# Plain weight rows only in the middle FFN stages, five of them and sooner; the next stage's first weights loaded at fixed places

## The chip, the cores and the metric

The kernel runs on one core of one Trainium2 chip. The metric is device time in microseconds of one execution; lower is better. TensorE (PE) multiplies, VectorE (DVE) and ScalarE (ACT) work on tiles in on-chip memory, GpSimd (POOL) and SyncE (SP) mostly issue transfers here. Each of these engines works through its own instructions in order, so an instruction that waits holds up all behind it on the same engine.

## The reference

A trunk of two layers over 512 tokens of width 1024, in float32. Each layer is an FFN, a mixing stage, and a second FFN, every one with its own RMS norm and its own shift, scale and gate computed from a vector c:

```python
for l in range(DEPTH):
    mod = (c_act @ w_ada[l] + b_ada[l]).reshape(B, N_MOD, D_MODEL)
    sh1, sc1, gt1, sh2, sc2, gt2, sh3, sc3, gt3 = [mod[:, i, None, :] for i in range(N_MOD)]
    hn = rms_norm(h, g_ffn1[l]) * (1.0 + sc1) + sh1
    h = h + 0.5 * (1.0 + gt1) * swiglu(hn, w_ffn1_in[l], w_ffn1_out[l])
    hn = rms_norm(h, g_mix[l]) * (1.0 + sc2) + sh2
    proj = hn @ w_mix_in[l]
    ...
    h = h + (1.0 + gt2) * mixed
    hn = rms_norm(h, g_ffn2[l]) * (1.0 + sc3) + sh3
    h = h + 0.5 * (1.0 + gt3) * swiglu(hn, w_ffn2_in[l], w_ffn2_out[l])
```

The FFN's hidden width is 2816: `swiglu(x) = (silu(gate) * up) @ w_out`. The mixing stage (attention in windows, a recurrent part, a short convolution) is not touched by the change, only the moments at which its first weights arrive.

## The kernel before

Activations lie transposed, features on the 128 partitions and the 512 tokens along the row. The six stages run one behind the other: FFN 1, mixing and FFN 2 of layer 0, then of layer 1. Every matmul is made three times in a reduced format: `split` (line 107 on ScalarE, line 108 on VectorE) turns a float32 tile into a high part `wH` and a low part `wL`, and TensorE adds up high by high, high by low and low by high. So each weight tile costs a load, a ScalarE copy and a VectorE subtraction before TensorE can use its last third.

The first FFN goes another way. The other three (second FFN of layer 0, first and second of layer 1) are made by `ffn_whole`, which cuts the weight matrix and the activations in two by two blocks and computes seven block products in place of eight. The first part of the stage takes eleven pairs of hidden blocks one by one (`pair_in`). The second part, `out_product`, multiplies the 22 hidden blocks by `w_out`; its seven products are, in order, A0, S, A1, S0, S1, S3 and A3, and each takes eleven rows of weights, in six units of two, two, two, two, two and one row. A row is 128 partitions by 512 numbers, 256 KB; a unit of two rows is 24 matmuls of 128 x 256 (four output blocks, two rows, three parts), so a row is 12 and a product 132. In the text "product five" is S1, "product six" is S3.

Four of the seven need sums of blocks. S is the sum of two blocks: SyncE loads the first (`sum`), GpSimd adds the second to it with an accumulating transfer. S0 adds A0's rows on VectorE. S1 adds a third block to S's buffers by another accumulating transfer, once S0's splits have read them. S3 adds a block to A0's kept rows (`rowk`), again by accumulating transfers of 256 KB each, with one exception: for the last three rows (8, 9, 10) the block is loaded plainly by SyncE (`Y`, line 836; its place in the table of due times is unit 20 of 42, line 912), and VectorE adds it at line 878, just ahead of that row's split. These are the "plain rows". Where the additions come in VectorE's own order is decided by the program's scheduler, and it may be well ahead of the split.

Loads are issued from a table: `dues` names the unit at which a load is issued, `prepare(t)` issues what is due and makes the splits of the unit two further on, `queued` holds the loads of one engine in that order. `wraw` is a pair of buffers through which loads pass to be split; `com`, `raw`, `sum` and others are buffers of the first part that come free.

Two of these three stages are followed by another one, whose first four weight tiles (W0 to W3 here) are loaded while `out_product` ends: two into `wraw`, one into a part of `spare`, the fourth into a buffer with the tag `raw` (named `wraws`, line 1044). The norm's statistics (`stats`, `spread`: a sum over partitions by TensorE, `ps_ss`, a root, and a broadcast) are woven into the last units of products six and seven; in this place the order of VectorE and ScalarE is written out by hand. The mixing stage then loads weights through `wraw` and, on GpSimd's queue, blocks of `w_ada` (`wada`) and a copy of silu(c) (`crow`), from which VectorE computes dot products (line 171) for later shifts and scales. ScalarE there makes `qr` and `qsq` from finished products, and TensorE's `ps_q` waits for the last of them.

Of the kernel before, what the change touches and what calls it, by code (L numbers as in the profile page):

```python
# [8 lines left out]
F32 = mybir.dt.float32  # L9
# [7 lines left out]
P = 128  # L17
# [46 lines left out]
def trunk_kernel(ctx, tc, ins, out, layers=L, phases=("ffn1", "mix", "ffn2")):  # L64
# [592 lines left out]
    def ffn_whole(l, w_in, w_pair, w_s, hn, im, ss, need, then, ready):  # L657
# [4 lines left out]
        with tc.tile_pool(name="act", bufs=1) as ap_:  # L662
# [65 lines left out]

            crow = []
# [5 lines left out]
            def pair_in(p):  # L735
# [19 lines left out]
                nc.gpsimd.dma_start(a00, A(1, 0), accum_op=ALU.add)  # L755
                if alone:
# [47 lines left out]

            def out_product(rest):
# [5 lines left out]
                tall = [slice(2 * u, min(2 * u + 2, NP)) for u in range(NU)]  # L811
                size = [s.stop - s.start for s in tall]
                S_, kept, late_rows, ready_, chain = {}, {}, {}, {}, {}

                def queued(eng, *args, **kw):
                    with queue_behind(chain.get(eng)):
                        chain[eng] = eng.dma_start(*args, **kw)
# [7 lines left out]
                def load(name, u):  # L825
# [6 lines left out]
                    elif name == "S3":  # L832
                        for k in ks:
                            if k not in late_rows:
                                queued(nc.gpsimd, kept[k], block(one(k), 1, 0), accum_op=ALU.add)
                    elif name == "Y":
                        for k in range(NP - 3, NP):
                            late_rows[k] = row_tile(k)
                            queued(nc.sync, late_rows[k], block(one(k), 1, 0))
                        return  # L840
# [3 lines left out]
                    if name == "A1":  # L844
                        w = wp.tile([P, KD, P], F32, name="wraw", tag="wraw", bufs=2)
                        queued(nc.sync, w[:, :n], block(tall[u], 0, 1))
                    elif name in ("S", "A3"):
                        if u < 5:
                            w = ap_.tile([P, KD, P], F32, name="sum", tag=("sum1", "crep", "first", "sum0", "third")[u], bufs=1)
                        else:  # L850
                            w = hnp.tile([P, 4, P], F32, name="rowk", tag="hn")
                        queued(nc.sync, w[:, :n], block(tall[u], 1, name == "A3"))
                        if name == "S":
                            S_[u] = w
                            queued(nc.gpsimd, w[:, :n], block(tall[u], 1, 1), accum_op=ALU.add)
# [1087 lines left out]
```

## Time and profile before

| | us |
|---|---|
| three runs | 1884.57, 1883.04, 1878.89 |
| median | 1883.04 |
| profiled execution | 1887.26 |
| its span, first to last instruction | 1885.5 |
| mean granted TensorE clock | 0.990 of full |
| out_product of the second FFN of layer 0 | about 835 to 955 |
| out_product of the first FFN of layer 1 | about 1170 to 1290 |
| out_product of the second FFN of layer 1 (last) | about 1755 to 1886 |

All places in the trace are microseconds from the span's start. A row of a list of waits reads: engine, tile and line that waited, what it waited for, the sum, how often, the longest. A row of a timeline: start, length, engine, line, operation, output and inputs, shape, and in square brackets the idle time ahead of it with what ended it. A row of a table by stretches: the stretch, its length, busy time of PE, PE's weight loads, DVE, ACT and POOL with instructions in brackets, then the granted clock, the mean share of the 16 DMA engines, and GB/s. DMA rows in a chain of waits run from issue to arrival. A row of one engine's name with q behind it is the time to issue.

### The profile page before, as it was taken

What the parts mean: (1) busy time and instruction counts of PE and PEld (TensorE: products, weight loads), DVE (VectorE), ACT (ScalarE), POOL (GpSimd) and SP (SyncE); (2) the same over time, 40 slices, a digit from 0 to 9 for tenths busy, and PEclk for the clock granted to TensorE, in tenths of its full rate; (3) what the DMA queues carried; (4) which work ended last, traced back from release to release, by engine and by line L of the source; (5) the groups of instructions that cost most, each with busy time, mean ns of one, the idle gap of its engine ahead of it and who ended that gap; (6) DMA issues with size and microseconds to landing.
All of it is one profiled execution on the core that took longest, in us unless ns stands there. A gap on an engine that the chain in (4) does not pass through costs nothing.

```text
span 1885.5 us, 39610 instructions
## 1 busy us (share of the span) xinstructions
PE 1836.2 (97%) x16468; PEld 1747.0 (93%) x16468; DVE 1538.5 (82%) x2443; ACT 919.7 (49%) x1413; POOL 185.8 (10%) x274
## 2 busy tenths in 40 slices
PE   9999999999999999999999999999999999999979
PEld 8998899888889999999999999999777999999979
DVE  6897687868886889999888998887597778877875
ACT  4453255346342545555654555564553335555544
POOL 0101110100000011110211111021000001110120
PEclk8999999999999999999999999999999999999989
DMA  8666876541212488876738987572211317765772
GB/s 315 215 201 227 273 198 220 187 149 46 75 44 87 132 266 262 256 211 179 177 111 271 267 252 214 172 185 106 88 54 49 103 51 221 199 168 132 199 177 92
DMA packets 112212, 322.01 MB, mean 171 GB/s; under 512 B 24096, under 2 KB 29216, under 8 KB 111008
## 3 DMA queue, kind: packets, MB, share of 16 engines
q1 hardware_dynamic: 74880, 192.06, 29.1%
q0 software_dynamic: 37152, 127.42, 27.6%
q8 instruction: 129, 2.11, 0.4%
q14 instruction: 51, 0.42, 0.1%
HBM read 315.50 MB, written 3.93 MB: 169 GB/s over the span
## 4 chain that ended last, share of the span: by engine, by line
PE 72%; DVE 16%; DMA 7%; issue 2%; ACT 2%; SPq 0%; DVEq 0%; ACTq 0%; POOL 0%; POOLq 0%
PE ps_mm L104 14%; PE ps_d L724 5%; PE ps_d L726 5%; PE ps_d L725 5%; PE ps_d L931 5%; PE ps_mm L97 4%; PE ps_mm L96 4%; PE ps_mm L98 4%; DVE wL L108 3%; DMA rowk<-in_w2s 3%; PE ps_f L724 2%; PE ps_f L725 2%; PE ps_f L726 2%; PE ps_g L931 2%; PE ps_f L931 2%
## 5 line engine op out<-in xcount | busy, mean ns | idle before, releaser
L107 ACT CAST wH<-wraw 128x1024 fp32r<-128x1024 f32 (+2 forms) x210 | 207.1, 988 | 318.6 <-PE ps_f L725 58.3
L108 DVE TENSOR_TENSOR wL<-wraw,wH 128x1024 fp32r<-128x1024 f32 (+2 forms) x210 | 238.7, 1140 | 54.1 <-ACT wH L107 53.7
L107 ACT CAST wH<-sum 128x1024 fp32r<-128x1024 f32 x153 | 161.0, 1052 | 141.0 <-PE ps_d L725 62.6
L108 DVE TENSOR_TENSOR wL<-sum,wH 128x1024 fp32r<-128x1024 f32 x153 | 186.7, 1220 | 36.4 <-ACT wH L107 35.5
L104 PE MATMUL ps_mm<-hnH,wL 128*128 128x256 f32 x976 | 199.1, 282 | 1.3 <-DVE wL L108 1.3
L104 PE MATMUL ps_mm<-hnH,wH 128*128 128x256 f32 x976 | 198.2, 283 | 0.5 <-ACT wH L107 0.3
L104 PE MATMUL ps_mm<-hnL,wH 128*128 128x256 f32 x976 | 196.7, 281 | 0.0
L726 PE MATMUL ps_d<-comH,wL 128*128 128x256 f32 x648 | 179.0, 276 | 0.6 <-DVE wL L108 0.6
L724 PE MATMUL ps_d<-comH,wH 128*128 128x256 f32 x648 | 179.2, 277 | 0.0
L725 PE MATMUL ps_d<-comL,wH 128*128 128x256 f32 x648 | 178.9, 276 | 0.0
L104 PEld LDWEIGHTS ps_mm<-hnH,wH 128*128 128x128 f32 x976 | 149.0, 188 | 9.8 <-issue 6.8
L104 PEld LDWEIGHTS ps_mm<-hnH,wL 128*128 128x128 f32 x976 | 149.7, 189 | 6.7 <-issue 4.6
L104 PEld LDWEIGHTS ps_mm<-hnL,wH 128*128 128x128 f32 x976 | 149.4, 189 | 5.9 <-issue 5.8
L931 PE MATMUL ps_d<-xs,wH 128*128 128x256 f32 x792 | 135.5, 276 | 0.0
L726 PEld LDWEIGHTS ps_d<-comH,wL 128*128 128x128 f32 x648 | 121.6, 188 | 0.8 <-DVE wL L108 0.8
L724 PEld LDWEIGHTS ps_d<-comH,wH 128*128 128x128 f32 x648 | 121.6, 188 | 0.2
L725 PEld LDWEIGHTS ps_d<-comL,wH 128*128 128x128 f32 x648 | 121.7, 188 | 0.0
L931 PEld LDWEIGHTS ps_d<-xs,wH 128*128 128x128 f32 x792 | 119.3, 188 | 0.0
L931 PE MATMUL ps_d<-xs,wL 128*128 128x256 f32 x396 | 109.7, 277 | 4.0 <-DVE wL L108 4.0
L931 PE MATMUL ps_f<-xs,wH 128*128 128x256 f32 x528 | 93.2, 281 | 0.0
L171 DVE SCALAR_TENSOR_TENSOR raw<-raw,crow 128x1024 f32<-128x1024 f32 x68 | 82.7, 1216 | 6.0 <-DMA raw<-in_wadaT 4.9
L171 DVE SCALAR_TENSOR_TENSOR wada<-wada,crep 128x1024 f32<-128x1024 f32 x60 | 71.8, 1220 | 17.2 <-DMA wada<-in_wadaT 17.2
(550 smaller groups left out, 5590.7 us busy)
## 6 DMA issues: line engine op xcount, KB each, us to landing
raw<-in_wadaT POOLq DMA_DIRECT2D x68, 512.0 KB, 6.4
wada<-in_wadaT POOLq DMA_DIRECT2D x60, 512.0 KB, 4.9
wraw<-in_wmi SPq DMA_DIRECT2D x38, 512.0 KB
wraw<-in_w2p SPq DMA_DIRECT2D x36, 512.0 KB
wraw<-in_w1p SPq DMA_DIRECT2D x32, 512.0 KB
sum<-in_w2s SPq DMA_DIRECT2D x20, 512.0 KB
sum<-in_w2s POOLq DMA_DIRECT2D x20, 512.0 KB, 9.1
wraw<-in_w1i SPq DMA_DIRECT2D x18, 512.0 KB
```

Of the source, the lines that this page charges most:

```text
L96: mm(acc, wH, xH, start=start, stop=False)
L97: mm(acc, wH, xL, start=False, stop=False)
L98: mm(acc, wL, xH, start=False, stop=stop)
L104: mm(acc[:, sl], w[a][:, k], x[b][:, sl], start=start and n == 0 and sl is HALVES[0], stop=stop and n == 2, skip_group_check=True)
L107: nc.scalar.copy(hi, src)
L108: return nc.vector.tensor_sub(lo, src, hi.bitcast(F32))
L171: stt(w, w, 1.0, crep, ALU.mult, ALU.mult, accum_out=out_)
L724: mm(pt[:, i], wH, x[k][0], start=start and i + k == 0, stop=False, skip_group_check=True)
L725: mm(pt[:, i], wH, x[k][1], start=False, stop=False, skip_group_check=True)
L726: last = mm(pt[:, i], wL, x[k][0], start=False, stop=k == 3, skip_group_check=True)
L931: mm(pt[m // 2][:, m % 2], w[:, 4 * k + m], x[:, y, k], start=start and u + k + n + m % 2 == 0, stop=u == NU - 1 and n == 2, skip_group_ch ...
```

## The change

1. Plain rows. The last stage has none now: all eleven rows of S3 come by accumulating transfers. The two stages in the middle have five (rows 6 to 10): rows 8, 9 and 10 are due at unit 8, rows 6 and 7 together in one `wraw` buffer at unit 16. Before, all three stages had three, at unit 20.
2. The sums for the first two units of S are issued in the last input pair (`sum_of`) instead of after it; the buffers of the five sums change places.
3. A1's units 2 and 3 get two buffers of `com` instead of waiting for `wraw`; all of A1's due times are new.
4. The next stage's first weights have fixed places in the order: W2 at unit 10, W0 at unit 17, W1 two units before the end of product six, W3 two units after it. W3 goes through `wraw`, no longer through `raw`.
5. `stats` and `spread` of the first half come one unit later.

VectorE's order in the last stage, from the end of S0's splits to S1's second, first before:

```order
L108 TENSOR_TENSOR xs<-raw,xs 128x512
L108 TENSOR_TENSOR wL<-sum,wH 128x1024
L108 TENSOR_TENSOR xs<-raw,xs 128x512 x2
L108 TENSOR_TENSOR wL<-rowk,wH 128x512
L108 TENSOR_TENSOR xs<-raw,xs 128x512
L878 TENSOR_TENSOR rowk<-rowk 128x512 x3
L108 TENSOR_TENSOR wL<-sum,wH 128x1024
L108 TENSOR_TENSOR xs<-raw,xs 128x512
L108 TENSOR_TENSOR wL<-sum,wH 128x1024
```

and now:

```order
L108 TENSOR_TENSOR xs<-raw,xs 128x512
L108 TENSOR_TENSOR wL<-sum,wH 128x1024
L108 TENSOR_TENSOR xs<-raw,xs 128x512 x2
L108 TENSOR_TENSOR wL<-rowk,wH 128x512
L108 TENSOR_TENSOR xs<-raw,xs 128x512
L108 TENSOR_TENSOR wL<-sum,wH 128x1024
L108 TENSOR_TENSOR xs<-raw,xs 128x512
L108 TENSOR_TENSOR wL<-sum,wH 128x1024
```

The three additions of plain rows are gone from between S0's last split (`wL<-rowk`) and S1's first.

SyncE's order in the second FFN of layer 0, from A1's loads to the next stage's weights (`in_w1i`), first before:

```order
L817 DMA wraw<-in_w2s 128x1024 x2
L308 DMA raw<-in_w1i 128x1024
L817 DMA wraw<-in_w2s 128x1024 x3
L817 DMA wraw<-in_w2s 128x512
L817 DMA rowk<-in_w2s 128x512 x3
L308 DMA wraw<-in_w1i 128x1024 x2
L817 DMA sum<-in_w2s 128x1024 x5
L817 DMA rowk<-in_w2s 128x512
L308 DMA wraw<-in_w1i 128x1024 x2
L308 DMA wraws<-in_w1i 128x1024
```

and now:

```order
L815 DMA wraw<-in_w2s 128x1024 x4
L815 DMA rowk<-in_w2s 128x512 x3
L815 DMA raw<-in_w1i 128x1024
L815 DMA wraw<-in_w2s 128x1024
L815 DMA wraw<-in_w2s 128x512
L815 DMA wraw<-in_w2s 128x1024
L815 DMA wraw<-in_w1i 128x1024
L815 DMA sum<-in_w2s 128x1024 x5
L815 DMA rowk<-in_w2s 128x512
L815 DMA wraw<-in_w1i 128x1024 x2
```

The three plain rows (`rowk` x3) moved ahead of A1's last two units, a transfer for rows 6 and 7 (the third `wraw<-in_w2s`) came in behind those, and only one of the next stage's `wraw` loads is now ahead of A3's sums instead of two.

VectorE at the start of layer 1's mixing stage, from W3's split (`wraws` before), first before:

```order
L108 TENSOR_TENSOR wL<-wraws,wH 128x1024
L295 SCALAR_TENSOR_TENSOR hnL<-hn_t,mod_3_9410,hnH 128x256
L1158 TENSOR_SCALAR om<-par 128x8
L1159 TENSOR_SCALAR w0h<-par 128x2
L1160 TENSOR_SCALAR a0h<-par 128x2
L1161 TENSOR_TENSOR gqk<-par 128x1
L108 TENSOR_TENSOR wL<-wraw,wH 128x1024
L1184 RECIPROCAL rk<-rk 128x512
L171 SCALAR_TENSOR_TENSOR wada_15646,mod_7_13740<-wada_15646,crow_15645 128x1024
```

and now:

```order
L108 TENSOR_TENSOR wL<-wraw,wH 128x1024
L295 SCALAR_TENSOR_TENSOR hnL<-hn_t,mod_3_9410,hnH 128x256
L171 SCALAR_TENSOR_TENSOR wada_15650,mod_7_13742<-wada_15650,crow_15649 128x1024
L108 TENSOR_TENSOR wL<-wraw,wH 128x1024
L171 SCALAR_TENSOR_TENSOR wada_15651,mod_7_13742<-wada_15651,crow_15649 128x1024
L1213 RECIPROCAL rk<-rk 128x512
```

The first dot product over `wada`, which needs `crow`, now stands ahead of the second weight split instead of behind it.

The diff, cut to its core:

```diff
-    def load_w(src, n=KD, raw=None, pair=None):
+    def load_w(src, n=KD, raw=None, pair=None, here=False):
...
-        loads.append(nc.sync.dma_start(w[:, :n], src))
+        if not here:
+            loads.append(nc.sync.dma_start(w[:, :n], src))
...
-    def ffn_whole(l, w_in, w_pair, w_s, hn, im, ss, need, then, ready):
+    def ffn_whole(l, w_in, w_pair, w_s, hn, im, ss, upcoming, then, ready):
...
                 nc.gpsimd.dma_start(a00, A(1, 0), accum_op=ALU.add)
+                if p == NP - 1:
+                    for u in range(2):
+                        sum_of(u)
...
+            def sum_of(u):
+
+                n, src = 4 * size[u], [w_s[l, 1, kh, :, tall[u]].rearrange("p k m c -> p (k m) c") for kh in range(2)]
+                if u < 5:
+                    S_[u] = ap_.tile([P, KD, P], F32, name="sum", tag=("sum1", "third", "crep", "first", "sum0")[u], bufs=1)
+                else:
+                    S_[u] = hnp.tile([P, 4, P], F32, name="rowk", tag="hn")
+                queued(nc.sync, S_[u][:, :n], src[0])
+                queued(nc.gpsimd, S_[u][:, :n], src[1], accum_op=ALU.add)
+                ready_["S", u] = [S_[u][:, :n]]
...
+                    elif name == "Y" and u < 4:
+                        w = wp.tile([P, KD, P], F32, name="wraw", tag="wraw", bufs=2)
+                        queued(nc.sync, w[:, :n], block(tall[u], 1, 0))
+                        late_rows.update((k, w[:, 4 * m : 4 * m + 4]) for m, k in enumerate(ks))
+                        return
                     elif name == "Y":
-                        for k in range(NP - 3, NP):
+                        for k in ks:
                             late_rows[k] = row_tile(k)
                             queued(nc.sync, late_rows[k], block(one(k), 1, 0))
+                        return
+                    elif name == "W":
+                        early[u] = wp.tile([P, KD, P], F32, name="wraw", tag="wraw", bufs=2) if u != 2 else flat(spare[3]).rearrange("p (k c) -> p k c", c=P)
+                        queued(nc.sync, early[u], upcoming[u])
...
                     if name == "A1":
-                        w = wp.tile([P, KD, P], F32, name="wraw", tag="wraw", bufs=2)
+                        pool, tag, bufs = (ap_, "com", 8) if u in (2, 3) else (wp, "wraw", 2)
+                        w = pool.tile([P, KD, P], F32, name="wraw", tag=tag, bufs=bufs)
...
-                dues = {-6: [("A0", u) for u in range(3)] + [("S", u) for u in range(3)] + [("A0", 3), ("S", 3)] + [("A0", 4), ("A0", 5), ("S", 4), ("S", 5)]}
+                early = {}
+                dues = {-6: [("A0", u) for u in range(3)] + [("S", 2)] + [("A0", 3), ("S", 3)] + [("A0", 4), ("A0", 5), ("S", 4), ("S", 5)]}
...
-                    due = 0 if name == "A1" and u < 2 else min(t - ahead_of[name], 6 * NU - 3)
+                    due = {0: 0, 1: 0, 2: 6, 3: 6}.get(u, t - 4) if name == "A1" else min(t - ahead_of[name], 6 * NU - 3)
...
-                dues.setdefault(20, []).insert(0, ("Y", 0))
+                if upcoming:
+                    for t, *what_ in ((8, ("Y", 4), ("Y", 5)), (10, ("W", 2)), (16, ("Y", 3)), (17, ("W", 0))):
+                        dues.setdefault(t, []).extend(what_)
...
                 with tc.manual_schedule(engines=HAND):
+                    load("W", 1)
                     prepare(end - 2)
-                    ahead(0, raws[0])
+                    ahead(0, early[0], True)
...
-                    ahead(2, raws[2])
-                    stats(hi_)
+                    ahead(2, early[2], True)
                     prepare(end + 1)
                     nothing(end + 1)
-                    spread(hi_)
+                    stats(hi_)
+                    load("W", 3)
                     prepare(end + 2)
                     nothing(end + 2)
+                    spread(hi_)
...
-                    raws.append(ap_.tile([P, 2, KD, P], F32, name="wraws", tag="raw", bufs=NU)[:, 0])
...
-                    ahead(3, raws[3])
+                    ahead(3, early[3], True)
...
-                marks = ffn_whole(l, ins[w + "i"], ins[w + "p"], ins[w + "s"], hn, im, nss, need, then, ready)
+                marks = ffn_whole(l, ins[w + "i"], ins[w + "p"], ins[w + "s"], hn, im, nss, first_weights(n + 1) if nss else (), then, ready)
```

`upcoming` is the list of the next stage's first four weight tiles; it is empty in the last stage, so the plain rows and the W loads are left out there.

More of the change, by code (lines that the diff above doesn't have):

```diff
@@ L727, in prod @@
                 return last
+            tall = [slice(2 * u, min(2 * u + 2, NP)) for u in range(NU)]
+            size = [s.stop - s.start for s in tall]
             crow = []
@@ L803, in pair_in, with queued @@
                 waiting.append(rest)
+            S_, chain, ready_ = {}, {}, {}
+            def queued(eng, *args, **kw):
+                with queue_behind(chain.get(eng)):
+                    chain[eng] = eng.dma_start(*args, **kw)
+            def sum_of(u):
[7 more added lines that the diff above has]
+                ready_["S", u] = [S_[u][:, :n]]
             def out_product(rest):
@@ L810, in out_product @@
                 pD, pF, pG = ([psum([P, 2, H2], n, t) for _ in range(2)] for n, t in (("ps_d", "x"), ("ps_f", "mm"), ("ps_g", "r0")))
[L811 to L817, printed above, removed]
+                kept, late_rows = {}, {}
                 def block(ks, mh, kh):
@@ L844, in load @@
                     if name == "A1":
-                        w = wp.tile([P, KD, P], F32, name="wraw", tag="wraw", bufs=2)
+                        pool, tag, bufs = (ap_, "com", 8) if u in (2, 3) else (wp, "wraw", 2)
+                        w = pool.tile([P, KD, P], F32, name="wraw", tag=tag, bufs=bufs)
                         queued(nc.sync, w[:, :n], block(tall[u], 0, 1))
-                    elif name in ("S", "A3"):
+                    elif name == "A3":
                         if u < 5:
-                            w = ap_.tile([P, KD, P], F32, name="sum", tag=("sum1", "crep", "first", "sum0", "third")[u], bufs=1)
+                            w = ap_.tile([P, KD, P], F32, name="sum", tag=("sum1", "third", "crep", "first", "sum0")[u], bufs=1)
                         else:
                             w = hnp.tile([P, 4, P], F32, name="rowk", tag="hn")
[L852 to L855, printed above, removed]
+                        queued(nc.sync, w[:, :n], block(tall[u], 1, 1))
                     else:
@@ L1000, in out_product @@
                 silu = im == 6
-                raws = [wp.tile([P, KD, P], F32, name="wraw", tag="wraw", bufs=2) for _ in range(2)]
-                raws.append(flat(spare[3]).rearrange("p (k c) -> p k c", c=P))
                 def update(q, ms):
@@ L1022, in out_product @@
                 with tc.manual_schedule(engines=HAND):
+                    load("W", 1)
                     prepare(end - 2)
-                    ahead(0, raws[0])
+                    ahead(0, early[0], True)
                     prepare(end - 1)
-                    ahead(1, raws[1])
+                    ahead(1, early[1], True)
                     nothing(end - 2)
@@ L1665, in normed, with first_weights @@
         return norm(l, g, im, im + 1, ss, n > 1 and seq[n - 1][1] != "mix")
+    def first_weights(n):
+        l, p = seq[n]
+        if p == "mix":
+            return [ins["wmi"][l, k] for k in range(4)]
+        return [ins["w1i" if p == "ffn1" else "w2i"][l, *divmod(k, 2)] for k in range(4)]
     def begin(pool):
@@ L1836, in then @@
             scale()
-            l2, p2 = seq[n + 1]
-            if p2 == "mix":
-                srcs = [ins["wmi"][l2, k] for k in range(4)]
-            else:
-                srcs = [ins["w1i" if p2 == "ffn1" else "w2i"][l2, *divmod(k, 2)] for k in range(4)]
-            return steps + [lambda k, raw: ws.append(load_w(srcs[k], KD, raw))]
+            srcs = first_weights(n + 1)
+            return steps + [lambda k, raw, here=False: ws.append(load_w(srcs[k], KD, raw, None, here))]
         if p == "mix":
```

3 lines of the change are left out of this document (added).

## The prediction

> **What bounds the kernel now.** I read the page first. TensorE is busy nearly everywhere, so only its gaps, and stretches at a lower clock, can give time back.
>
> ```profile
> PE 1836.2 (97%) x16468; PEld 1747.0 (93%) x16468; DVE 1538.5 (82%) x2443; ACT 919.7 (49%) x1413; POOL 185.8 (10%) x274
> ```
>
> Then I asked for TensorE's waits in the three stages that the diff touches and at the start of the mixing stage behind one of them. First the last stage (1750 to 1886 us):
>
> ```profile
> PE ps_f L931 <- DVE wL L108: 9.8, 2, 9.5
> PE ps_d L931 <- DVE wL L108: 0.8, 1, 0.8
> PE ps_g L931 <- DVE wL L108: 0.7, 2, 0.4
> ```
>
> One wait of 9.5 us stands out; the rest of the three rows is 0.3 + 0.8 + 0.7 = 1.8 us. It stands at the start of product five (S1, into `ps_f`). VectorE's timeline shows why `wL` was late, SyncE's and the chain of waits what it waited for:
>
> ```profile
> 1826.95 0.69 DVE L878 TENSOR_TENSOR rowk<-rowk 128x512 f32<-128x512 f32 x1 [8.87 <-DMA rowk<-in_w2s]
> 1831.55 1.22 DVE L108 TENSOR_TENSOR wL<-sum,wH 128x1024 fp32r<-128x1024 f32 x1
> 1814.79 3.70 SPq L817 DMA_DIRECT2D rowk<-in_w2s  x3
> 1816.82 14.10 DMA rowk<-in_w2s
> 1832.82 17.93 PE ps_f L931 x130
> 1850.75 9.29 PE ps_d L931 x82
> ```
>
> VectorE works in order. The three additions of plain rows (one row for the first) stand ahead of the split that S1 needs, and the rows were issued at 1814.79 and arrived up to 14.1 us later. The sums for S1 were there; the split only stood behind. The stall also costs clock. The stretches, with the granted clock third from the end:
>
> ```profile
> 1820.00:1830.00 10.00, 3.33 (x30) 3.13 (x28) 1.39 (x2) 3.43 (x5) 5.69 (x7) 0.77 1.07 240
> 1830.00:1840.00 10.00, 7.18 (x37) 7.18 (x38) 9.06 (x13) 1.56 (x2) 0.00 (x0) 0.55 1.08 224
> 1855.00:1870.00 15.00, 15.00 (x133) 15.00 (x132) 11.57 (x18) 8.96 (x14) 0.00 (x0) 1.00 0.58 203
> ```
>
> At the full clock 133 matmuls take 15.00 us, 0.113 each, so the 130 of S1 should take 14.66; they took 17.93. The clock cost 3.3 us on top of the 9.5. The Trainium skill ("TensorE: Matmul & The Clock Gate", Part 1) has the clock come back after about 3.4 us of busy work; by that estimate only 1.7 us would be lost here and the sum below would be 1.6 us smaller. The row decides for 3.3.
>
> The two middle stages, second FFN of layer 0 (830 to 960), then first FFN of layer 1 (1170 to 1290):
>
> ```profile
> PE ps_d L931 <- DVE wL L108: 1.7, 1, 1.7
> PE ps_g L931 <- DVE wL L108: 0.7, 2, 0.5
> PE ps_ss L268 <- DVE ss L1016: 0.6, 1, 0.6
> ```
>
> ```profile
> PE ps_d L931 <- DVE wL L108: 1.5, 1, 1.5
> PE ps_g L931 <- DVE wL L108: 1.0, 2, 0.8
> PE ps_f L931 <- DVE wL L108: 0.8, 1, 0.8
> PE ps_ss L268 <- DVE ss L1016: 0.6, 1, 0.6
> ```
>
> That is 3.0 and 3.9 us, 6.9 together. Last, the start of layer 1's mixing stage (1290 to 1340), and the same wait in layer 0 (400 to 420):
>
> ```profile
> PE ps_q L1206 <- ACT qsq L1200: 3.1, 1, 3.1
> ```
>
> ```profile
> PE ps_q L1206 <- ACT qsq L1200: 1.1, 1, 1.1
> ```
>
> and what the clock did behind the longer one:
>
> ```profile
> 1328.50:1331.50 3.00, 2.63 (x12) 1.76 (x12) 0.59 (x1) 0.91 (x2) 0.00 (x0) 0.83 0.84 269
> 1331.50:1337.30 5.80, 5.80 (x27) 4.42 (x25) 1.21 (x3) 0.29 (x1) 0.00 (x0) 0.50 0.11 42
> ```
>
> Layer 1 waits 2.0 us longer, and then works 5.8 us at half clock and 3.0 at 0.83: 2.9 + 0.5 = 3.4 us more. In all 5.4 us hang on this place.
>
> **The change, part by part.** *Last stage, no plain rows.* The three VectorE additions go, and with them everything that stood ahead of the split at 1831.55. Worth 9.5 + 3.3 = 12.8. Of the 1.8 us of small waits I take two thirds, 1.2, since two sums come earlier and two A1 units get buffers of their own; bounds 0 and 1.8. The cost is that all eleven rows of S3 are now added up by GpSimd's accumulating DMAs, where eight were. Is that in time?
>
> ```profile
> 1829.01 0.87 POOL L817 DMA_DIRECT2D rowk<-in_w2s  x1 [1.20 <-DMA rowk<-in_w2s]
> rowk<-in_w2s POOLq DMA_DIRECT2D x9, 256.0 KB, 13.2
> ```
>
> The eighth row was issued at 1829.01 and by the median of its group (13.2 us, in the answer on DMA from 1809 to 1842) landed near 1842.2: eight rows in 13.2 us, 1.65 each. Three more make 1847.2. The plain rows' 0.75 MB no longer run in the same full window; at the 224 to 240 GB/s of the two stretches above they took 3.3 us, so the last row lands near 1843.9, and with its cast and split (0.62 and 0.69 us, in rows quoted below) is ready at 1845.2. TensorE reaches the last two units of S3 at 1850.75 - 12.8 - 1.2 + 8 rows x 12 matmuls x 0.113 = 1847.6. It fits by 2.4 us; cost 0, with the miss as a rival below. Part: **14.0**.
>
> *Middle stages, five plain rows, sooner.* Product six waits 1.7 and 1.5 us at its last rows. The chain there (stage of layer 0):
>
> ```profile
> 910.47 16.40 DMA rowk<-in_w2s
> 933.66 0.39 PE L931 MATMUL ps_d<-xs,wL 128*128 128x256 f32 x1 [1.69 <-DVE wL L108]
> ```
>
> Eight accumulating rows took 16.4 us, 2.05 each; VectorE's splits of the last three rows stand behind the eighth in its order. With six, that chain ends 4.1 us sooner, more than the wait: I take 2.7 of 3.2. For it VectorE gets two more additions per stage, 2 x 0.69 = 1.4 us. It has no room in that stretch, but some just ahead:
>
> ```profile
> 860.00:885.00 25.00, 24.70 (x213) 24.17 (x212) 24.68 (x38) 14.87 (x22) 0.00 (x0) 1.00 0.35 98
> 885.00:910.00 25.00, 24.55 (x216) 24.35 (x215) 25.00 (x39) 17.85 (x27) 11.42 (x13) 1.00 0.97 212
> 835.00:860.00 25.00, 25.00 (x221) 24.93 (x220) 21.27 (x36) 14.47 (x24) 5.19 (x6) 1.00 1.04 294
> 850.46 0.69 DVE L108 TENSOR_TENSOR wL<-rowk,wH 128x512 fp32r<-128x512 f32 x1 [2.15 <-ACT wH L107]
> 853.74 0.69 DVE L108 TENSOR_TENSOR wL<-rowk,wH 128x512 fp32r<-128x512 f32 x1 [1.05 <-ACT wH L107]
> 849.81 0.62 ACT L107 CAST wH<-rowk 128x512 fp32r<-128x512 f32 x1 [2.27 <-DMA rowk<-in_w2s]
> ```
>
> VectorE is full from 860 to 910, but idled 2.15 + 1.05 = 3.2 us before, behind rows of A0 that came late while the DMA share was 1.04. The first two sums (1 MB plain and 1 MB accumulating) leave that window for the last input pair, so most of the 3.2 comes back: 1.8 net of the additions. It meets waits of 0.7 and 1.8 us in products two and three; I take 1.5 of 2.5. The statistics matmul moves one unit's end later, about five matmuls or 0.6 us: 0.8 of the 1.2. What the early sums can cost: GpSimd now issues two accumulating sums ahead of the pair's own.
>
> ```profile
> 818.53 0.88 POOL L755 DMA_DIRECT2D first<-in_w2p  x1 [8.06 <-DVE wL L108]
> 829.60 1.06 ACT L107 CAST wH<-first 128x1024 fp32r<-128x1024 f32 x1 [1.18 <-issue]
> ```
>
> That load has 11.1 us from issue to use; two sums in front are four rows' worth, 4 x 2.05 = 8.2 us if none of it was done by 818.53, beside its own two rows' 4.1. So 0 to 1.2 us in each of three stages; I take 0.5 in all. Part: 2.7 + 1.5 + 0.8 - 0.5 = **4.5**, bounds 0 and 6.9.
>
> *The next stage's weights at fixed places.* The fourth weight tile W3 moves from a buffer tagged `raw` to `wraw`. The loads for layer 1's mixing were late because of what was ahead:
>
> ```profile
> 1302.63 1.62 POOL L212 DMA_DIRECT2D wada<-in_wadaT  x3 [58.97 <-DVE hnL L295]
> 1311.79 1.22 DVE L171 SCALAR_TENSOR_TENSOR wada<-wada,crow 128x1024 f32<-128x1024 f32 x1 [0.98 <-DMA crow<-silu_c]
> 1306.17 6.69 DMA wraw<-in_wmi
> 1321.23 1.05 ACT L107 CAST wH<-wraw 128x1024 fp32r<-128x1024 f32 x1 [6.31 <-DMA wraw<-in_wmi]
> ```
>
> In the old order the first `wada` load is held until after W3's split; in the new one it follows the last product, some 12 us sooner, so its 2 MB with `crow` no longer run beside the weights of 1306 and VectorE's dot no longer waits for `crow`. ScalarE, whose `qr` and `qsq` stand behind the casts in its order, is then less late. The wait can fall to layer 0's 1.1 and the half clock vanish: 5.4. It can also stay as it is, since two buffers still limit the weights: 0. The 6.69 us of that load, against a need of 2.0 us less, lies nearer the first; I take **3.3**.
>
> *Sum.* 14.0 + 4.5 + 3.3 = 21.8 us. The profiled execution took 1887.26 us (span 1885.5), 4.2 above the median 1883.04. It becomes about 1865.5; on the median **1861**.
>
> **Rivals.** (a) *Only the last stage gains.* VectorE stays the bound in the middle stages, its two additions eating the relief, and the mixing start is limited by its two buffers. For it: 25.00 of 25 us busy. Against: the wait at product six follows a DMA, not VectorE's load. Time: 1883 - 12.8 = 1870.
>
> (b) *The stall moves to product six of the last stage.* At the middle stages' 2.05 us per row, eleven rows from 1828.7 (when the sixth sum was in, by the issue at 1829.01) land at 1851.3, with 1.3 for cast and split 5.0 us after 1847.6; the clock falls again for 3.3. Net 21.8 - 8.3 = 13.5: 1869.5. Against: the middle stages load A3's and the next stage's weights beside, the last only A3's. The Trainium skill ("DMA: Bandwidth & Descriptors", Issuing engines are not separate DMA queues) says that transfers of all issuing engines share the same sixteen DMA engines, so making plain rows accumulating ones frees no DMA time by itself; the share of 1.07 and 1.08 above agrees, and the rival stands on that.
>
> (c) *Slower: the plain rows are late in both middle stages instead.* Y3 (rows 6 and 7) is loaded through `wraw`, behind the split of A1's fifth unit, and its additions stand in VectorE's order in front of S0's and S1's splits, as in the last stage now. If each stalls as that did (12.8), the two cost 25.6 against 14.0 won and nothing else: 1883 + 11.6 = 1895. It decides from 7.0 us of stall and clock per stage. Against: eight VectorE rows, some 8 us, lie between that split and the addition, and in that window (860 to 885) the DMA share is 0.35.
>
> (d) *It does not do what it says at the mixing start*: `wada` is held by something else, and the dot, now ahead of a weight split that ran at 1304.92 before, blocks VectorE until 1311.8, about 7 us. Then 21.8 - 3.3 - 7 = 11.5: 1871.5.
>
> **How the numbers follow.** Forecast 0.60, (a) 0.20, (b) 0.08, (d) 0.06, (c) 0.05; 0.01 for the rest. Everything at its best is 12.8 + 1.8 + 6.9 + 5.4 = 26.9, so 1856; the three runs of before lie 4.2 us under and 1.5 over their median, so low 1853. The high end takes in (a), (b) and (d): 1874. About 0.3%, 5.6 us, is what a measurement of this kernel can tell from no change. All cases but (c) are beyond it; some of (a) and (d) can add up to less, so faster 0.91, same 0.04, slower 0.05.
>
> **What would show it.** Right: no wait over 1 us at the start of S1 in the last stage and a granted clock of 1.00 from 1815 to its end; S3's last casts there not held by a DMA for more than 2 us; VectorE's idle time at the start of the middle out-products gone and product six's 1.7 and 1.5 gone; `wada` issued near 1290 less the gains, `ps_q` waiting about 1 us. Wrong: a new wait at `ps_d` in the last stage (b), additions of plain rows held by a DMA in the middle stages (c), a wait of a mixing dot for `crow` (d), or a cast of `first` late in the last input pair.

## The result, and the profile after

| | before | changed |
|---|---|---|
| median of the runs, us | 1882.9 (1878.89 to 1884.57) | 1854.17 (1850.88 to 1858.96) |
| profiled execution, us | 1887.26 | 1850.88 |
| its span, us | 1885.5 | 1849.1 |

The ratio is 0.9853, 95% interval 0.9835 to 0.9871: 28.7 us faster on the medians. The forecast was 1861 us, 21.8 faster, in a range of 1853 to 1874. The side and the range held; the gain was a third larger than the sum.

The first row of the page, and the waits of TensorE in the last stage (1720 to 1850) and at the mixing start of layer 1 (1260 to 1310):

```profile
PE 1822.6 (99%) x16468; PEld 1739.3 (94%) x16468; DVE 1538.2 (83%) x2444; ACT 921.3 (50%) x1413; POOL 184.4 (10%) x273
```

```profile
PE ps_g L961 <- DVE h L968: 0.6, 1, 0.6
PE ps_d L725 <- DVE up L797: 0.2, 1, 0.2
```

```profile
PE ps_ks L1146 <- ACT ksq L1207: 0.8, 1, 0.8
PE ps_ss L268 <- DVE ss L1044: 0.2, 1, 0.2
```

The 9.5 us at `ps_f` and the 3.1 us at `ps_q` are gone; what is left was there before too, but for the 0.2 at `ps_d`. For the two middle out-products (830 to 960 and 1160 to 1285) the same question has one row, the same in both:

```profile
PE ps_ss L268 <- DVE ss L1044: 0.2, 1, 0.2
```

Of the seven rows shown before, five are gone, and the two of the statistics fell from 0.6 to 0.2 us each. VectorE does the same work as before, 1538 us busy. TensorE's idle time fell from 49.3 to 26.5 us of the span, and its busy time by 13.6 us for the same 16468 matmuls, mostly because less of them ran at half clock: the mean granted clock rose from 0.990 to 0.999.

The chain of waits through products four to six of the last stage is TensorE alone, and S1 takes 132 matmuls x 0.1133 = 14.96 us, the full clock. Then GpSimd's issues of S3's rows (the first and the last two of the list; the first of its seven is still S1's), the median time to arrival of all twelve, and ScalarE's casts of the last rows:

```profile
1784.97 14.39 PE ps_d L961 x127
1799.37 14.96 PE ps_f L961 x132
1814.33 10.77 PE ps_d L961 x95
```

```profile
1791.91 6.20 POOL L815 DMA_DIRECT2D rowk<-in_w2s  x7 [0.95 <-DVE wL L108]
1805.46 0.86 POOL L815 DMA_DIRECT2D rowk<-in_w2s  x1 [0.39 <-DMA rowk<-in_w2s]
1806.75 0.86 POOL L815 DMA_DIRECT2D rowk<-in_w2s  x1 [0.42 <-DMA rowk<-in_w2s]
rowk<-in_w2s POOLq DMA_DIRECT2D x12, 256.0 KB, 11.8
```

```profile
1812.89 1.14 ACT L107 CAST wH<-rowk 128x512 fp32r<-128x512 f32 x2 [1.27 <-PE ps_f L961]
1816.97 1.14 ACT L107 CAST wH<-rowk 128x512 fp32r<-128x512 f32 x2 [0.95 <-PE ps_d L961]
1819.69 0.62 ACT L107 CAST wH<-rowk 128x512 fp32r<-128x512 f32 x1 [1.06 <-PE ps_d L961]
```

The casts wait for TensorE to give buffers back, none for a DMA: eleven accumulating rows are in time. GpSimd issues its last rows as earlier ones arrive, 1806.75 - 1805.46 = 1.3 us apart, less than the 1.65 that the forecast took.

The start of layer 1's mixing stage, on GpSimd, VectorE and by stretches:

```profile
1276.33 1.61 POOL L212 DMA_DIRECT2D wada<-in_wadaT  x3 [48.32 <-PE ps_g L961]
```

```profile
1288.65 1.22 DVE L171 SCALAR_TENSOR_TENSOR wada<-wada,crow 128x1024 f32<-128x1024 f32 x1
```

```profile
1300.00:1310.00 10.00, 10.00 (x91) 9.87 (x92) 3.77 (x5) 3.44 (x6) 0.53 (x1) 1.00 0.67 237
1310.00:1320.00 10.00, 10.00 (x73) 7.39 (x72) 4.64 (x13) 2.67 (x5) 0.00 (x0) 1.00 0.19 63
```

`wada` is issued when the last product ends, 26 us sooner than before (13 of them are the stage's own earlier end); the dot does not wait for `crow`; TensorE is busy throughout these 20 us, at the full clock.

Where the time went shows best in stretches between the same matmuls, counted in order of time, of the profiled execution of each run (all have 16468 matmuls). They are worked out from the starts of the matmuls in the trace. They lie around the out-product of layer 0's second FFN (matmul 7201 to 8341), that of layer 1's first FFN (10141 to 11001), the mixing start behind it (11001 to 11431) and the last out-product (15461 to the last matmul); the rest, from the first matmul on, is what the change does not touch apart from a wait or two. A stretch does not begin and end exactly with its product, but it holds the same matmuls in every run.

| us | middle, layer 0 | middle, layer 1 | mixing start | last | rest |
|---|---|---|---|---|---|
| before | 136.1 | 105.2 | 60.2 | 132.6 | 1445.5 |
| changed | 134.9 | 98.4 | 54.0 | 116.2 | 1439.7 |
| changed, again (`e9_after`) | 131.3 | 98.4 | 54.0 | 116.2 | 1441.4 |
| `e1_last_none` | 136.4 | 104.3 | 61.3 | 117.9 | 1443.1 |
| `e2_last_three` | 131.3 | 98.4 | 54.0 | 126.8 | 1447.4 |
| `e3_w3_raw` | 134.9 | 98.4 | 61.1 | 119.8 | 1444.7 |
| `e4_late_sums` | 134.9 | 98.4 | 54.2 | 119.8 | 1444.7 |
| `e5_three_rows` | 132.7 | 100.8 | 54.0 | 116.3 | 1440.0 |
| `e6_a1_wraw` | 134.9 | 98.1 | 54.2 | 119.6 | 1448.3 |
| `e10_both` | 135.1 | 99.1 | 54.2 | 116.8 | 1440.9 |
| `e11_rows_only` | 136.6 | 104.5 | 58.4 | 119.6 | 1443.4 |
| `e12_old_tags` | 134.4 | 101.3 | 54.1 | 119.4 | 1444.6 |
| `e13_rows_tags` | 135.3 | 101.8 | 56.7 | 117.3 | 1442.7 |

Of the 36.4 us between the two profiled executions 5.8 lie in the rest, 4.7 of them in the first 80 us, which no edit touches. 30.6 us lie in the four stretches: 1.2 + 6.8 + 6.2 + 16.4.

### The profile page after: what moved, and what is told of

The parts are those of the page before. It is cut to its first block, busy times and chain, and to the rows that moved or that the text cites. A ratio compares the mean times of both kernels' runs of the same rounds, so it can differ in the third digit from the quotient of the medians.

```text
span 1849.1 us, 39606 instructions
## 1 busy us (share of the span) xinstructions
PE 1822.6 (99%) x16468; PEld 1739.3 (94%) x16468; DVE 1538.2 (83%) x2444; ACT 921.3 (50%) x1413; POOL 184.4 (10%) x273
## 4 chain that ended last, share of the span: by engine, by line
PE 83%; DVE 12%; ACT 2%; DMA 2%; issue 1%; SPq 0%; POOL 0%; DVEq 0%; ACTq 0%
PE ps_mm L104 15%; PE ps_d L961 7%; PE ps_d L725 5%; PE ps_d L727 5%; PE ps_d L726 5%; PE ps_g L961 5%; PE ps_f L961 5%; PE ps_mm L97 4%; PE ps_mm L96 4%; PE ps_mm L98 4%; PE ps_f L727 3%; PE ps_f L725 3%; PE ps_f L726 3%; PE ps_d L495 1%; PE ps_d L496 1%; PE ps_d L497 1%
## 5 line engine op out<-in xcount | busy, mean ns | idle before, releaser
L961 PEld LDWEIGHTS ps_d<-xs,wH 128*128 128x128 f32 x792 | 119.6, 188 | 0.0
```

The source lines that it names most:

```text
L961: mm(pt[m // 2][:, m % 2], w[:, 4 * k + m], x[:, y, k], start=start and u + k + n + m % 2 == 0, stop=u == NU - 1 and n == 2, skip_group_ch ...
```

## The experiments

**The last stage, with the plain rows taken out of the old kernel.** The edit of `e1_last_none`:

```diff
-                dues.setdefault(20, []).insert(0, ("Y", 0))
+                if ss is not None:
+                    dues.setdefault(20, []).insert(0, ("Y", 0))
```

> The kernel before, with one part of the change alone: no plain rows in the last stage, its eleven rows of S3 all by accumulating transfers. Theory A (the three additions of plain rows, standing ahead of S1's split in VectorE's order, made the 9.5 us wait and the half clock behind it): the wait at ps_f in the last stage is gone, the granted clock stays at 1.00 there, and the time falls by 12.8 us, to 1870; the waits of the middle stages (3.0 and 3.9 us) and ps_q's 3.1 us stay. Rival B (the wait came from a DMA window that was too full, and the early sums cured it): the wait stays above 5 us and the time falls by less than 6 us. Rival C (eleven accumulating rows are late): a new wait of about 5 us at ps_d in product six, time about 1876.

1870.61 us against 1880.97 of the kernel before on the same chip, ratio 0.9945 (0.993 to 0.9961). The waits of its last stage (1745 to 1872) and the chain through it:

```profile
PE ps_g L932 <- DVE h L939: 0.6, 1, 0.6
PE ps_g L932 <- DVE wL L108: 0.4, 1, 0.4
```

```profile
1804.18 14.96 PE ps_d L932 x132
1819.14 14.96 PE ps_f L932 x132
1834.10 14.96 PE ps_d L932 x132
```

No wait at S1, the full clock, and no new wait at S3 (rival C falls): theory A. The stretch is 14.7 us shorter, 12.8 of it foretold; the medians of whole executions differ by 10.4 only. The waits of the middle stages were to stay; layer 1's sum to 3.4 us in the list, layer 0's to 1.6, without the 1.7 at `ps_d`. That product ran in the slow rhythm told of below, and the gap there was 152 ns against 1969 before: a wait that is missing in a slow stretch need not have been cured.

**And put back into the changed kernel** (`e2_last_three`):

```diff
+                else:
+                    dues.setdefault(20, [])[:0] = [("Y", 4), ("Y", 5)]
```

> The changed kernel, with three plain rows put back in the last stage alone, at the old place in the order (unit 20). Theory A: the wait at S1's start in the last stage comes back with about 9 us and half a clock behind it, 12 to 13 us in all, time about 1867. Rival B (early sums and A1's own buffers cured it): the plain rows come sooner now, the wait is under 4 us and the time is within 5 us of 1854.

1865.16 us, ratio to the kernel before 0.9913 (0.9883 to 0.9943); the last stretch is 10.6 us longer than in the changed kernel. VectorE's timeline, TensorE's wait, the chain, and two stretches of S1:

```profile
1805.23 0.69 DVE L905 TENSOR_TENSOR rowk<-rowk 128x512 f32<-128x512 f32 x1 [8.89 <-DMA rowk<-in_w2s]
1809.24 0.69 DVE L905 TENSOR_TENSOR rowk<-rowk 128x512 f32<-128x512 f32 x1 [1.36 <-DMA rowk<-in_w2s]
1809.85 1.22 DVE L108 TENSOR_TENSOR wL<-sum,wH 128x1024 fp32r<-128x1024 f32 x1
```

```profile
PE ps_f L963 <- DVE wL L108: 7.4, 1, 7.4
```

```profile
1794.66 14.55 DMA rowk<-in_w2s
1811.12 17.24 PE ps_f L963 x130
```

```profile
1811.10:1814.80 3.70, 3.68 (x17) 3.68 (x18) 3.70 (x6) 0.00 (x0) 0.00 (x0) 0.50 1.12 207
1814.80:1828.40 13.60, 13.60 (x117) 13.60 (x117) 10.72 (x18) 7.36 (x13) 0.00 (x0) 1.00 0.24 63
```

The same picture as before the change: rows 14.55 us on the way, additions ahead of the split, 7.4 us of waiting, and S1 slower by 17.24 - 14.66 = 2.6 us. Not all of that is clock: S1's first 17 matmuls start 213 ns apart at half clock, which costs 1.9 us; the others start 117.8 ns apart at full clock, the slow rhythm told of below, which costs 0.5. The rhythm goes on behind S1 and takes another 1 us or so of the 10.6, so the additions alone cost about 9 us here, less than the 12 to 13 foretold. The two runs together show that the additions' place is the cause, and that neither the early sums nor A1's buffers cure it (rival B falls). The wait is 2 us shorter than in the kernel before; which of the other edits does that was not tried.

**W3's buffer** (`e3_w3_raw`):

```diff
-                    load("W", 3)
...
+                    early[3] = ap_.tile([P, 2, KD, P], F32, name="wraws", tag="raw", bufs=NU)[:, 0]
...
-                    ahead(3, early[3], True)
+                    ahead(3, early[3])
```

> The changed kernel, with the fourth first weight (W3) back in the buffer tagged raw, loaded at the end of the product as before. Theory A (W3's buffer held wada, and with it the weights of the mixing start): wada is issued about 12 us later again, behind W3's split, ps_q waits about 3 us again in layer 1 and the clock falls to half behind it; 5 to 6 us slower, about 1860. Rival B (the 6 us came from the earlier end of the stage and its own loads, not from W3's buffer): within 2 us of 1854.

1862.55 us, ratio to the kernel before 0.9899 (0.9878 to 0.992); the mixing start takes 61.1 us against 54.0. Its waits, GpSimd's row and two stretches:

```profile
PE ps_q L1235 <- ACT qsq L1229: 3.1, 1, 3.1
```

```profile
1293.94 1.61 POOL L212 DMA_DIRECT2D wada<-in_wadaT  x3 [60.90 <-DVE hnL L295]
```

```profile
1321.00:1327.00 6.00, 6.00 (x24) 4.65 (x24) 1.21 (x3) 0.87 (x2) 0.00 (x0) 0.54 0.24 87
1327.00:1332.00 5.00, 5.00 (x28) 4.55 (x28) 2.64 (x12) 0.12 (x1) 0.00 (x0) 0.53 0.00 0
```

One buffer's tag brings all of it back: `wada` behind W3's split, 3.1 us at `ps_q`, and about 11 us near half clock (0.54 and 0.53). Theory A holds.

**Which edit emptied the middle stages.** `e4_late_sums` loads the first two sums behind the last pair again, `e6_a1_wraw` gives A1's units two and three back to `wraw`, `e10_both` does the two together, and `e12_old_tags` also puts the buffers of the sums (and of A3's loads, which follow them) back in their old order. The first two hunks below are the edit of `e4_late_sums`, the next two that of `e6_a1_wraw`; `e10_both` has all four, `e12_old_tags` all five:

```diff
-                if p == NP - 1:
-                    for u in range(2):
-                        sum_of(u)
-                dues = {-6: [("A0", u) for u in range(3)] + [("S", 2)] + [("A0", 3), ("S", 3)] + [("A0", 4), ("A0", 5), ("S", 4), ("S", 5)]}
+                dues = {-6: [("A0", u) for u in range(3)] + [("S", u) for u in range(3)] + [("A0", 3), ("S", 3)] + [("A0", 4), ("A0", 5), ("S", 4), ("S", 5)]}
...
-                        pool, tag, bufs = (ap_, "com", 8) if u in (2, 3) else (wp, "wraw", 2)
+                        pool, tag, bufs = (ap_, "com", 8) if () else (wp, "wraw", 2)
...
-                    due = {0: 0, 1: 0, 2: 6, 3: 6}.get(u, t - 4) if name == "A1" else min(t - ahead_of[name], 6 * NU - 3)
+                    due = {0: 0, 1: 0}.get(u, t - 4) if name == "A1" else min(t - ahead_of[name], 6 * NU - 3)
...
-                    S_[u] = ap_.tile([P, KD, P], F32, name="sum", tag=("sum1", "third", "crep", "first", "sum0")[u], bufs=1)
+                    S_[u] = ap_.tile([P, KD, P], F32, name="sum", tag=("sum1", "crep", "first", "sum0", "third")[u], bufs=1)
```

> The changed kernel, with the first two sums of S loaded after the last input pair again, as before. Theory A (the early sums gave VectorE back some 3 us of idle time ahead of its full stretch): VectorE idles again for 2 to 3 us at the start of the middle out-products, and waits of 1 to 2 us come back in products two and three of both middle stages; 2 to 4 us slower, about 1857. Rival B (the five plain rows and A1's own buffers carry the middle stages): no wait over 0.5 us in them, time within 1 us of 1854.

1860.87 us, ratio to the kernel before 0.9889 (0.9865 to 0.9913). VectorE idles again at the start of the middle stage of layer 0:

```profile
849.55 0.69 DVE L108 TENSOR_TENSOR wL<-rowk,wH 128x512 fp32r<-128x512 f32 x1 [0.89 <-ACT wH L107]
852.82 0.69 DVE L108 TENSOR_TENSOR wL<-rowk,wH 128x512 fp32r<-128x512 f32 x1 [1.03 <-ACT wH L107]
```

In the changed kernel there is no such idle time. But TensorE waits nowhere for it, and the stretch of layer 1 is 98.4 again: on the waits, rival B. Its time, within 1 us of 1854, was missed. In the profiled execution the longer time lies in the rest (5 us) and in the last stretch, which ran in the slow rhythm. `e3_w3_raw`, whose edit reaches neither place, has both: 3.9 us more than the changed kernel between matmuls 600 and 7201, 4.0 in this run, each with half the clock from 533 to 540 us, and 119.8 us in the last stretch. So neither needs the late sums; whether they have a part in the median all the same stays open.

> The changed kernel, with A1's units two and three loaded through wraw again, as before. The run with late sums had no waits in products two and three, so the early sums are not what removed them. Theory A (A1's two buffers of its own let VectorE split them earlier): waits of 1 to 2 us come back at ps_g in product three of both middle stages and the last stage; out-product of layer 1's first FFN 1 to 2 us longer than 98.4. Rival B (the new due times of the rest, and the three fewer or earlier plain rows, carry it): no wait over 0.5 us there.

One execution, 1862.66 us: no wait for a split in either middle stage, 98.1. Rival B again; here too the time is in the rest and in the slow rhythm. In this run, in `e4_late_sums` and in `e10_both` layer 0's stage ran in the slow rhythm, so layer 1's, at 113 ns, decides.

> The changed kernel with two parts undone together: the first two sums after the last input pair, and A1's units two and three through wraw. Each alone left no wait in products two and three. Theory A (either is enough, they cover for one another): with both undone waits of 0.5 to 1.5 us come back at ps_g in product three and at ps_f in product two of the middle stages, and the out-product of layer 1's first FFN takes 1 to 3 us more than 98.4. Rival B (neither mattered; the plain rows' and the weights' new places in the order removed these waits): no wait over 0.5 us there, 98.4 again.

One execution, 1853.64 us: one wait of 0.3 us in the middle stage of layer 1, 99.1. Nearer to rival B; the two do cover for one another, but for 0.7 us.

> The run with both parts undone (late sums, A1 through wraw), and now also the five sums' buffers in the old order, so that the second sum waits for crep again in place of third. Theory A (which buffers the sums take set when they come, and that is what removed the waits in products two and three): waits of 0.5 to 1 us come back there in the middle stages, out-product of layer 1's first FFN at 100 to 102 us against 99.1. Rival B (the next stage's weights at fixed places removed them): 99 again, no wait over 0.5 us.

One execution, 1861.4 us. The waits of the middle stage of layer 1 (1170 to 1270):

```profile
PE ps_g L958 <- DVE wL L108: 0.7, 2, 0.5
PE ps_f L958 <- DVE wL L108: 0.4, 1, 0.4
```

101.3 us: 2.2 more than `e10_both`, 2.9 more than the changed kernel, and not by the slow rhythm, which took little of this stretch. So with the other two undone, undoing the order of the sums' buffers costs most; early sums and A1's own buffers are further covers for the same wait. Undone alone, each of these two costs nothing; the order was not undone alone, and each number is one execution's.

**The number of plain rows.** `e5_three_rows` leaves out rows 6 and 7:

```diff
-                    for t, *what_ in ((8, ("Y", 4), ("Y", 5)), (10, ("W", 2)), (16, ("Y", 3)), (17, ("W", 0))):
+                    for t, *what_ in ((8, ("Y", 4), ("Y", 5)), (10, ("W", 2)), (17, ("W", 0))):
```

> The changed kernel, with three plain rows instead of five in the middle stages (rows 8 to 10, still at unit 8), so that S3 has eight accumulating rows there as before. Theory A (the eighth accumulating row held product six): the wait at ps_d near the end of product six comes back in both stages, 1 to 2 us each, so the profiled out-product of layer 1's first FFN is 1 to 2 us longer than the changed kernel's 98.4. Rival B (the plain rows' earlier place, or W0's later one, cured it): no wait over 0.5 us there.

One execution, 1851.47 us. The waits of its two middle stages, layer 0 first:

```profile
PE ps_d L961 <- DVE wL L108: 0.7, 1, 0.7
```

```profile
PE ps_d L961 <- DVE wL L108: 1.8, 1, 1.8
```

They are back, with nothing else changed, and the stretch of layer 1 is 2.4 us longer: theory A. That the whole execution was no slower than the changed kernel's shows how little a single time tells here.

`e11_rows_only` makes the plain rows' part alone in the kernel before (five and sooner, none at the end), and `e13_rows_tags` adds the sums' new buffers. The edit of the first:

```diff
+                        if u == 3:
+                            w = wp.tile([P, KD, P], F32, name="wraw", tag="wraw", bufs=2)
+                            queued(nc.sync, w[:, :n], block(tall[u], 1, 0))
+                            late_rows.update((k, w[:, 4 * m : 4 * m + 4]) for m, k in enumerate(ks))
...
-                dues.setdefault(20, []).insert(0, ("Y", 0))
+                if ss is not None:
+                    for t, *what_ in ((8, ("Y", 4), ("Y", 5)), (16, ("Y", 3))):
+                        dues.setdefault(t, []).extend(what_)
```

> The kernel before with the plain rows' part alone: five and sooner in the middle stages, none in the last; sums, A1 and the next weights as they were. Theory A: product six waits for nothing any more in the middle stages (1.7 and 1.5 us gone), but VectorE's two more additions make the waits in products two and three as large as before or larger (0.7 and 1.8 us, plus up to 1.4); out-product of layer 1's first FFN 103 to 105 us against 105.2; last stage about 117, as in the run with that part alone. Rival B (the rows' earlier place relieves VectorE too): products two and three without waits over 0.5 us, out-product of layer 1's first FFN at 99 to 101.

One execution, 1870.02 us. Middle stage of layer 1 (1167 to 1272):

```profile
PE ps_g L938 <- DVE wL L108: 0.8, 1, 0.8
PE ps_f L938 <- DVE wL L108: 0.5, 1, 0.5
PE ps_g L938 <- ACT wH L107: 0.4, 1, 0.4
```

Products two and three wait about as long as before, as theory A has it (104.5 us). Product six (`ps_d`) no longer waits, but that shows nothing here: from 1217 to 1272 us this stage ran in the slow rhythm, in which layer 0's product six of `e1_last_none` had no wait either, with the old rows. That the rows cure product six rests on `e5_three_rows`, whose middle stages ran at 113 ns.

> The kernel before with the plain rows' part and the new order of the sums' buffers, nothing else. Theory A (the buffers' order): the waits in products two and three (0.5, 0.4 and 0.8 us in layer 1's first FFN with the rows alone) fall under 0.3 each, out-product there at 101 to 102 us against 104.5. Rival B (the next stage's weights at fixed places): they stay, 104 to 105.

One execution, 1861.46 us: 101.8 and no wait there, but all of that stretch ran in the slow rhythm, in which VectorE has more time per product. It cannot tell the buffers from the rhythm: inconclusive. In layer 0's stage a wait of 0.5 us at `ps_g` stands in both runs, with the old order of the buffers and with the new.

**The slow rhythm.** In the changed kernel's profile the middle stage of layer 0 won only 1.2 us although its waits were gone. Its matmuls follow one another more slowly. The stretch from 840 to 930, the changed kernel first, then the same kernel again (`e9_after`):

```profile
840.00:930.00 90.00, 90.00 (x767) 90.00 (x766) 83.27 (x130) 57.03 (x89) 12.23 (x14) 1.00 0.65 172
```

```profile
840.00:930.00 90.00, 90.00 (x796) 90.00 (x796) 86.55 (x135) 57.90 (x90) 12.23 (x14) 1.00 0.68 181
```

767 matmuls against 796 in the same 90 us, at the same granted clock of 1.00, without a wait: the gaps between starts are 117.9 ns against 113.3.

> The changed kernel itself again, as what the others of this call are compared with: 1854 us, 1851 to 1859; the out-products without waits, and the slow rhythm of 118 ns per matmul in none, one or two of them, not always the same ones if it is a matter of chance.

1855.5 us (1849.04 to 1857.72), ratio to the kernel before 0.9869 (0.984 to 0.9898); no out-product in the slow rhythm this time, so it is not the program alone that decides.

`e8_break` puts a short matmul ahead of the second unit of products one to five:

```diff
+                        if q < 5 and u == 1:
+                            (wH, wL), x = ready_[q, u]
+                            mm(psum([P, T], "ps_nop", "r1")[:, :64], wH[:, 0], x[:, 0, 0, :64], start=True, stop=True)
```

> The changed kernel, with five small matmuls (64 columns, their result not used) put into each of the three out-products, one ahead of the second unit of products one to five. In the profile of the changed kernel the matmuls of the out-product of layer 0's second FFN follow one another every 117.9 ns from 838 to 940 us, in those of layer 1 every 113; the slow rhythm began behind a short wait of 0.16 us and lost 4 us. Theory A (a rhythm of weight loads and matmuls that holds until something breaks it): the small matmuls break it, no stretch of more than 40 us at 118 ns is left in any out-product, they cost about 0.1 us each, 1.5 us in all; where the changed kernel falls into the slow rhythm once or twice per run, the median is 2 to 5 us lower and the spread smaller. Rival B (the rhythm comes from what is read, from a memory or a buffer): the slow stretch stays and the time is 1.5 us longer.

1859.97 us, ratio to the kernel before 0.9892 (0.9864 to 0.992): 4.5 us slower than `e9_after` by the medians. Three stretches of its middle stage of layer 1, which ran at 113 ns in both profiled executions of the changed kernel:

```profile
1187.00:1220.00 33.00, 33.00 (x284) 33.00 (x283) 33.00 (x50) 20.54 (x31) 1.89 (x3) 1.00 0.35 91
1221.00:1236.00 15.00, 15.00 (x135) 15.00 (x134) 14.56 (x25) 9.53 (x15) 7.86 (x9) 1.00 1.06 207
1237.00:1270.00 33.00, 33.00 (x282) 33.00 (x281) 25.59 (x43) 21.02 (x38) 0.00 (x0) 1.00 0.43 141
```

33.00 / 284 = 116 ns, then 111, then 117. These stretches do not begin and end with the small matmuls; counted in the trace from each of the five to the next, the gaps between starts are 113.3, 117.8, 117.8 and 113.3 ns, and 117.8 behind the fifth. A single matmul can end the rhythm and can also start it. Theory A's picture holds, its cure does not: no slow stretch over 40 us is left in the middle stages, but the last stage had one of 57 us from 1796 on, and the time rose where 2 to 5 us less were foretold.

## Why the prediction was right, and where it was off

The three places that the forecast named are where the time came from, and each gave more than its term: 30.6 us in the four stretches, 28.7 on the medians, against 21.8. The forecast's own "everything at its best", 26.9 us, was exceeded as well. That 1854.17 still lies in the range is owed to its low end, which had been set 3 us below that best for the spread of the runs; so the side and the mechanisms were foreseen, and the range held with some luck.

*Last stage, 14.0 forecast, 16.4 measured in the profiled executions.* Mechanism shown from both sides (`e1_last_none`, `e2_last_three`). The removed part alone gave 14.7; 12.8 was the wait and the clock. The 1.2 of small waits was put down to the early sums and A1's buffers; in `e1_last_none`, which has neither, 0.4 of the 1.8 us is left, so most of them went with the plain rows. The other edits gave the further 1.7. The check on eleven accumulating rows (ready 2.4 us ahead) came out on the safe side: the last rows came 1.3 us apart and not 1.65. Whether that is because no plain rows ran beside them is not shown. Rival (b) fell with it. The clock's part stood at 3.3 by the row: S1's first 29 matmuls ran at half clock, 6.2 us. In `e2_last_three` it was 17 matmuls, 3.7 us, and about 1.9 lost. The Trainium skill ("TensorE: Matmul & The Clock Gate", Part 1) has the clock come back after about 3.4 us of busy work; the second run agrees with that, the first does not.

*Middle stages, 4.5 forecast, 8.0 measured, 11.6 without the slow rhythm.* This is the first term that was mis-sized. I took the 6.9 us in the lists of waits as the most there was; the stretches of `e9_after` are 4.8 and 6.8 us shorter than before. The lists count a wait only from a matmul's modelled end, 276 ns after its start where the next should start after 113, so every wait is some 0.16 us longer than its row, and a gap shorter than 276 ns is in no row. Counted in the trace from start to start, the gaps above 135 ns cost 4.3 and 6.5 us more before than in `e9_after`, nearly all of the 4.8 and 6.8. The 2.7 for product six was right in kind (`e5_three_rows` brings the wait back). The 0.8 for the statistics is what their two rows lost. The 1.5 for products two and three had a reason that was not enough: VectorE's idle time at the start did go, and without the early sums 1.9 of its 3.2 us return, but TensorE then waits no more than with them. The order of the sums' buffers, named in the change and costed at nothing by me, counted for more in the one sequence of undoing that was tried (`e12_old_tags`). How much the weights' new places hold of the rest was not separated.

*Mixing start, 3.3 forecast, 6.2 measured.* The second term that was mis-sized. `e3_w3_raw` shows the chain as it was drawn: W3's buffer, `wada`, the weights, `qsq`, half clock. I gave it six tenths of 5.4; all of it came, and the wait went to nothing rather than to layer 0's 1.1 us. The rule for choosing between the bounds was at fault: the chain had been traced to its first link, and that link moved 12 us against a need of 2, so the upper bound was the better choice here. Rival (d) fell: `crow` was there.

*Cost of the early sums, 0.5 forecast:* in the changed kernel's profile ScalarE's cast of `first` in layer 0 waits 2.7 us for its transfer, the sign that was named; in `e9_after` it does not. TensorE waits for it in neither, so no cost is seen. *Rival (a)* fell on the middle stages and the mixing start, *(c)* on the middle stages: the five additions of plain rows wait for no DMA.

## What to carry to other kernels

When an in-order engine has optional work in its queue that waits for a transfer, look at what stands behind it. Two ways out worked here: giving the work to a queue where nothing waits behind it (the last stage), and issuing the transfer long enough ahead that nothing waits for it (the middle stages); which is worth more was not compared. A buffer's tag can carry a stage's time: trace a late load back through whoever held its buffer. Here the whole chain went with its first link. And compare kernels that differ by a few us by stretches between the same matmuls, since one whole time moves by more than that from run to run.

## What was not expected of the hardware

A stream of 128 x 256 matmuls with a weight load each has two rhythms at the same granted clock: 113.3 and 117.9 ns. In the changed kernel's profile the slow one began behind a short disturbance in layer 0's stage, two gaps of 154 and 221 ns, and held for 855 matmuls, 101 us, 3.9 us lost. `e9_after` and the kernel before have the same two gaps at the same matmuls (152 and 221, 151 and 222 ns) and go on at 113. In the last stage of four of the variants (`e3_w3_raw`, `e4_late_sums`, `e6_a1_wraw` and `e11_rows_only`) it began at one and the same matmul, behind a short gap too, and held for 917. In the profile of the old kernel, full of waits, no stretch of it reaches 120 matmuls; in `e1_last_none`, whose middle stages have the old waits, one reaches 341. So part of what removed waits give can be handed back. The spread of whole times does not show it: 9.9 us among the changed kernel's eight runs (1849.04 to 1858.96), 10.0 among seven of the old kernel (1876.74 to 1886.73). What sets the rhythm is open.

The first 50 us also differ between executions. From 20 to 50 us, before and after the change, in code that the change does not touch:

```profile
20.00:50.00 30.00, 30.00 (x238) 29.50 (x238) 24.25 (x50) 8.93 (x13) 0.00 (x0) 0.89 0.69 279
```

```profile
20.00:50.00 30.00, 29.97 (x253) 26.97 (x251) 28.30 (x56) 13.09 (x20) 0.00 (x0) 1.00 0.68 277
```

The old kernel's profiled execution ran there at a granted clock of 0.89 and had lost nearly 5 us by 80 us; no edit touches this part.
